# Output pieces of a state-space layer started one a slot, four gate blocks side by side, and one silu for the later columns

## The chip, the cores and the metric

The kernel runs on one core of a Trainium2 chip. The metric is device time in microseconds (us) of one execution; less is better. Three runs of the kernel before took 902.46 to 907.09 us, with a median of 904.3 us.

## What is computed

Two residual layers over 256 tokens of width 2048, in float32. Layer 0 is grouped-query attention and lies outside the change. Layer 1 is a bidirectional diagonal state-space layer, cut here to what matters:

```python
u, z = split(h @ w_in, 2)                       # 2 x 2048 columns
y = scan_fwd(u) + scan_bwd(u) + d_skip * u      # 128 groups of 16 channels, 64 complex states
g = gelu(y)
y = g * sigmoid(g @ w_glu + b_glu)
y = y * silu(z)
x = layer_norm(alpha * x + y @ w_out)
```

## The kernel before, in words

Every product is made from three reduced-precision ones: the weights are loaded in **chunks** of 512 KB (`raw`, L157, on SP's DMA queue), ScalarE (ACT) rounds a chunk to its high part `wh` (L146), GpSimd (POOL) or VectorE (DVE) takes the difference `wl` (L148), and TensorE (PE) runs 24 matmuls on it (`chunk_ch`, L209 to L211). `plan1` writes down the order of the chunks of layer 1: 16 blocks of 128 columns of u, 16 of z, 8 blocks of 256 columns of the gate `w_glu`, then `w_out`.

After each chunk the kernel calls `step()`, so a **slot** is one chunk of matmuls. In a slot each lane (`in`, `scan`, `out`, `g`, `glu`) may start waiting tasks, up to its width, and moves its live tasks on by one `yield`. `until(test)` calls `step()` without a chunk until the test holds. This fixes the order in which instructions are written; the framework then makes each engine's queue from it, and may pull an instruction forward that it takes for ready while the engine would be idle.

Layer 1 goes as follows. Blocks of u go out to DRAM and come back in another layout; `in_task` turns them into the scan's input `V`. The scan (`scan_task`, L888 to L890 on DVE) runs in two batches, pieces 0 to 7 and 8 to 15 (`BATCH`), 62 columns each, 3 columns a slot. Meanwhile PE makes the z blocks, and ACT puts silu on each (L1034) into `z1`.

`OUT_LAG` slots after a batch's last column its eight `out_task`s are queued; the lane's width is `OUT_W` = 2. A piece's task starts with the copies of the forward and backward states into `su` (L908 on ACT; L909 on ACT for pieces 0 to 7, on DVE for 8 to 15) and the loads of `om` (L913) and `up` (L918). At every fourth piece it also loads the Toeplitz block `tr` with eight DMAs (L495) and turns it into `tt` with two ACT copies (L498). Two slots later come 48 small matmuls into `yps` (L933), one slot after that gelu (L938) into `yg`, which is written to `Gd` by ACT's queue (L939). A `g_task` reads `Gd` back as `gp` (L953, SP's queue), and five slots later splits it into the two parts of `gT` (L243 on ACT, L244 on DVE).

The gate's matmuls need `gT`: chunk c of a block needs pieces 4c to 4c+3. Before, the first two gate blocks run chunks 0 to 2 each, then wait for pieces 12 to 15, then run their chunks 3; the other six blocks run whole. `glu_task` adds sigmoid (L963) and the products with `z1` (L966 to L968).

Buffers that the text speaks of: `su` and `tr` share the tag `q4` (4 slots), `om` and the scan's input `im` share `im` (`NIM` = 2), `tt` has one buffer, `yps` three PSUM banks, `yg` two. Loads of `up` and `gp` and the write of `Gd` are 128 KB each.

Of the kernel before, what the change touches and what calls it, by code (L numbers as in the profile page):

```python
# [9 lines left out]
F32 = mybir.dt.float32  # L10
F32R = mybir.dt.float32r
I32 = mybir.dt.int32
AF = mybir.ActivationFunctionType
# [5 lines left out]
S = 256  # L19
D = 2048  # L20
KB = D // 128
# [4 lines left out]
C = 16  # L26
NP = 64
L = 4
# [3 lines left out]
NB = G // GB  # L32
PG = 8
NPIECE = G // PG
# [6 lines left out]
class Trunk:  # L41
# [153 lines left out]
        self.step()  # L195
        return parts

    def chunk_ch(self, ps, act, c):

        self.feed()  # L200
        nc, (ah, al) = self.nc, act
        wh, wl = self.parts.pop(self.cur)
        n = wh.shape[1]
        for kk in range(n):
            kb = n * c + kk
            for i in range(len(ps)):
                f = slice(i * 128, i * 128 + 128)
                o = ps[i][:, :S]
                nc.tensor.matmul(o, lhsT=wh[:, kk, f], rhs=ah[:, kb], start=kb == 0, stop=False)  # L209
                nc.tensor.matmul(o, lhsT=wh[:, kk, f], rhs=al[:, kb], start=False, stop=False)  # L210
                self.mm = nc.tensor.matmul(o, lhsT=wl[:, kk, f], rhs=ah[:, kb], start=False, stop=kb == KB - 1).ins  # L211
        self.cur += 1
        self.step()

# [272 lines left out]
    def toeplitz(self, b):  # L487

        nc, wk = self.nc, self.wk1
        raw = wk.tile([128, L, 16, C], F32, tag="q4", name="tr", bufs=self.Q4)  # L490
        with self.tc.issue_after(self.paced):
            for h in range(2):
                for tau in range(L):
                    src = self.Kd[b, h, :, 3 - tau:7 - tau].rearrange("c j e -> c (j e)")
                    nc.sync.dma_start(raw[h * 64 + tau:h * 64 + 64:L].rearrange("q j a e -> q (j a e)"), src)  # L495
        t = wk.tile([128, 16, C, L], F32, tag="tt", name="tt")
        for a in range(2):
            nc.scalar.copy(t[:, a * 8:a * 8 + 8], raw[:, :, a * 8:a * 8 + 8].rearrange("q t a e -> q a e t"))  # L498
        return t

    def columns(self, pool):
# [290 lines left out]
    def plan1(self):  # L792
        a = self.a
        W, WG, WO = a["w_in_ssm"][0], a["w_glu"][0], a["w_out_ssm"][0]
        self.first = len(self.chunks)
        self.plan_ch(W, 0)
        for b in range(2, 32):
            self.plan_one(W, b * 128)
        for b in range(2):
            self.plan_ch(WG, b * 256, 0, 3)  # L800
        for b in range(2):
            self.plan_ch(WG, b * 256, 3, 4)
        for b in range(2, 8):
            self.plan_ch(WG, b * 256)
        for nb in range(4):
            self.plan_tok(WO, nb * 512, nb == 3)
# [71 lines left out]
    def scan_task(self, p0, p1):  # L878

        v = self.nc.vector  # L880
        n, g0 = (p1 - p0) * PG, p0 % 8 * PG
        V = self.V[p0 // 8][:, :, :, g0:g0 + n]
        cf = self.coef[:, :, :, p0 * PG:p1 * PG]
        shp = [128, 2, 2, n]
        for c in range(1, NCH - 1):
            P = self.sc.tile([128, 512], F32, tag="scp", name="scp")[:, :4 * n].rearrange("q (e r g) -> q e r g", e=2, r=2)
            with self.urgent():
                v.tensor_tensor(P, cf, V[:, c - 1].unsqueeze(1).to_broadcast(shp), ALU.mult)  # L888
                v.tensor_tensor(V[:, c], V[:, c], P[:, 0], ALU.add)
                self.swept = v.tensor_tensor(V[:, c], V[:, c], P[:, 1, ::-1], ALU.add).ins  # L890
            yield
        t = self.now + self.OUT_LAG
        while self.now < t:
            yield
        for pc in range(p0, p1):
            self.add("out", self.out_task(pc))

    def out_task(self, pc):

        nc, v, wk = self.nc, self.nc.vector, self.wk1  # L900
        b, q = pc // 4, pc % 4
        V = self.V[pc // 8]
        gs = slice(pc % 8 * PG, pc % 8 * PG + PG)
        su = wk.tile([128, 2, PG, NCH], F32, tag="q4", name="su", bufs=self.Q4)
        f, r = slice(0, 64), slice(64, 128)
        nc.gpsimd.memset(su[f, :, :, 0:1], 0.0)
        nc.gpsimd.memset(su[r, :, :, NCH - 1:], 0.0)
        nc.scalar.copy(su[f, :, :, 1:], V[f, 0:NCH - 1, :, gs].rearrange("p s r g -> p r g s"))  # L908
        (v.tensor_copy if pc >= 8 else nc.scalar.copy)(su[r, :, :, :NCH - 1], V[r, NCH - 2::-1, :, gs].rearrange("p s r g -> p r g s"))  # L909
        self.flags.add(("su", pc))  # L910
        tag, bufs = ("im", self.NIM) if self.n_in == NPIECE and self.OMT else ("q4", self.Q4)
        om = wk.tile([128, 2, PG, C * L], F32, tag=tag, name="om", bufs=bufs)
        nc.sync.dma_start(om, self.OMd[pc])  # L913
        if q == 0:
            self.tt = self.toeplitz(b)
        tt = self.tt
        up = wk.tile([128, 4, NCH], F32, tag="up", name="up2", bufs=3)
        nc.sync.dma_start(up, self.Ud[pc].rearrange("h c t a k -> (h c t) a k"))  # L918
        yield
        yield  # L920
        ps = self.pm.tile([128, 512], F32, tag="pm", name="yps", bufs=self.npm)

        h = [slice(g % 2 * 64, g % 2 * 64 + 64) for g in range(PG)]
        o = [ps[h[g], g // 2 * NCH:g // 2 * NCH + NCH] for g in range(PG)]
        even, odd = range(0, PG, 2), range(1, PG, 2)
        jobs = [(g, None) for g in even] + [(g, ri) for ri in range(2) for g in range(PG)] + [(g, None) for g in odd]
        seen = set()
        with ExitStack() as order:
            for n, (g, ri) in enumerate(jobs):
                lhsT = tt[h[g], q * 4 + g // 2].rearrange("q e t -> q (e t)") if ri is None else om[:, ri, g]  # L930
                rhs = up[h[g], g // 2] if ri is None else su[:, ri, g]
                stop = ri is None if g % 2 else ri == 1
                m = nc.tensor.matmul(o[g], lhsT=lhsT, rhs=rhs, start=g % 2 not in seen, stop=stop, skip_group_check=True)  # L933
                seen.add(g % 2)
                order.enter_context(self.tc.issue_after(m.ins))
        yield
        yg = wk.tile([128, 4, NCH], F32, tag="yg", name="yg", bufs=2)
        nc.scalar.activation(yg.rearrange("p a k -> p (a k)"), ps[:, :S], AF.Gelu_apprx_tanh)  # L938
        nc.scalar.dma_start(self.Gd[pc].rearrange("(a h) c t k -> (h c t) a k", h=2), yg)  # L939
        self.add("g", self.g_task(pc), *[("su", p) for p in range(8)])  # L940
# [49 lines left out]
    def layer1(self, out):  # L990
        nc, v = self.nc, self.nc.vector
# [11 lines left out]
        h = (hT[:, 0], hT[:, 1])  # L1003
        ps = self.banks()
# [19 lines left out]
        for b in range(2, NPIECE):  # L1024
            if "open" not in self.flags and (self.idle("prep") or b == self.OPEN):
                self.open(ssm)
            ps = self.block_ch(h)
            self.taken(b, ps[0])
            self.add("in", self.in_task(b), "open")
        s2, wk = self.s2, self.wk1  # L1030
        self.z1 = self.mid.tile([128, KB, S], F32, tag="mid", name="z1")
        for b in range(NPIECE):
            ps = self.block_ch(h)
            nc.scalar.activation(self.z1[:, b], ps[0][:, :S], AF.Silu)  # L1034
        self.until(lambda: self.idle("scan"))
        self.psum(4)

# [1 line left out]
        act = (self.gT[:, 0], self.gT[:, 1])  # L1039
        yT = self.s0.tile([128, 2, KB, S], F32R, tag="s0", name="y2T")  # L1040
        y = (yT[:, 0], yT[:, 1])
        need = lambda c: self.until(lambda: all(("g", p) in self.flags for p in range(4 * c, 4 * c + 4)))
        two, gains = [self.banks(), self.banks()], []
        for ps in two:
            for c in range(3):
                need(c)
                self.chunk_ch(ps, act, c)
        need(3)
        for b in range(8):
            if b < 2:  # L1050
                ps = two[b]
                self.chunk_ch(ps, act, 3)
            else:
                ps = self.block_ch(act)
            if b >= 4:
                gains.append(wk.tile([128, 2, 512], F32, tag="q4", name="gains", bufs=self.Q4))
                self.load_gains(gains[-1], 0, b - 4)
            for i in range(2):
                self.add("glu", self.glu_task(2 * b + i, ps[i][:, :S], y))
        ready = lambda c: all(("y", f) in self.flags for f in (2 * c, 2 * c + 1))  # L1060
        src = lambda i, cs: [(0, 128, self.h1d[i, :, cs])]
        for nb in range(4):
            res = self.residual(nb, src, gains[nb])
            gains[nb] = wk.tile([128, 2, 512], F32, tag="q4", name="gains2", bufs=self.Q4)
            self.load_gains(gains[nb], 1, nb)
            if nb == 3:
                break
            ps = self.block_tok(y, ready)
# [39 lines left out]
            self.layer1(out)  # L1108

    Q4 = 4  # L1110
    JOIN = (1, 0)
    FIN = (('V', 'gg', 'gg', 'gg'), ('V', 'gg', 'vv', 'vv'))
    ONE = 0
# [11 lines left out]
    GLAG = 5  # L1125
    POOL = (1, 70)
    OUT_W = 2
    OUT_E = 1
    OMT = 1
    IN_EVERY = 1  # L1130
# [1 line left out]
    EACH = 2  # L1132
    NRAW = 4
    HP = 0
    NIM = 2
    BUDGET = 8
    OUT_LAG = 4
    IN_LAG = 1
    BATCH = (8, 16)
    NWH = 4  # L1140
# [48 lines left out]
```

## Time and profile before

| | us |
|---|---|
| median of three runs | 904.3 |
| the profiled execution | 909.47 |
| its span, first to last instruction | 907.5 |
| scan of the state-space layer, DVE | 509.8 to 648.8 |
| last block of z done on PE | 679.4 |
| gate matmuls on PE | 681.0 to 804.2 |

The profile is of one execution. Busy time is the union of an engine's instructions; an "idle before" time is put down to what ended it. The granted clock of TensorE is a share of 2.4 GHz. The times of windows, timelines and chains count from the span's start.

### The profile page before, as it was taken

To read this page: it belongs to the slowest core of one execution; us is meant where nothing else is said; L and a number is where in the kernel's file an instruction comes from. 1 tells how busy PE (TensorE), PEld (TensorE's weight loads), DVE (VectorE), ACT (ScalarE), POOL (GpSimd) and SP (SyncE) were. 2 spreads that over 40 slices of the span, in tenths; PEclk is the share of its full clock that TensorE was granted. 3 is DMA by queue.
4 is the path that set the end of the run, shared out by engine and by line. 5 is a ranking of instruction groups with operands and counts; after the bars stand their busy time and mean duration, and the time that the engine had idled before them with its cause. 6 is when DMAs were issued, how large, how long until landed. Compare 5 with 4: busy or idle time off the path is not lost.

```text
span 907.5 us, 18418 instructions
## 1 busy us (share of the span) xinstructions
PE 841.0 (93%) x7244; PEld 763.8 (84%) x7244; DVE 651.8 (72%) x1178; ACT 519.9 (57%) x743; POOL 262.7 (29%) x182
## 2 busy tenths in 40 slices
PE   5999999999999898997889999998998789999993
PEld 4788989889899687886889999987897789998882
DVE  3999899999979977987200498899732477766646
ACT  3554467768668564454456566489968554543321
POOL 0008500000002222334556666744584000000004
PEclk9999999999999999998999999997999979999997
DMA  9765588776757658987789989774797946786733
GB/s 235 235 193 176 141 254 265 204 194 217 203 180 205 192 157 240 234 284 232 215 233 282 274 246 301 208 208 140 212 277 238 298 133 203 232 242 215 246 92 92
DMA packets 217798, 195.82 MB, mean 216 GB/s; under 512 B 67648, under 2 KB 174064, under 8 KB 217456
## 3 DMA queue, kind: packets, MB, share of 16 engines
q1 hardware_dynamic: 200688, 189.93, 70.3%
q10 hardware_dynamic: 17024, 4.72, 2.2%
q8 instruction: 57, 0.93, 0.4%
q14 instruction: 29, 0.24, 0.1%
HBM read 168.39 MB, written 26.21 MB: 214 GB/s over the span
## 4 chain that ended last, share of the span: by engine, by line
PE 64%; DMA 16%; DVE 8%; ACT 4%; issue 4%; SPq 2%; POOL 1%; ACTq 0%; DVEq 0%; POOLq 0%
PE acc L185 9%; PE acc L186 9%; PE acc L184 9%; PE acc L209 9%; PE acc L210 9%; PE acc L211 9%; DMA Ud<-ut 3%; DMA om<-OMd 2%; PE yps L933 2%; DMA up<-Ud 1%; DMA Gd<-yg 1%; PE kps L459 1%; DMA h1d<-r 1%; ACT su L908 1%; PE imps L441 1%
## 5 line engine op out<-in xcount | busy, mean ns | idle before, releaser
L146 ACT CAST wh<-raw 128x1024 fp32r<-128x1024 f32 x234 | 245.0, 1050 | 219.7 <-PE acc L186 74.1
L148 POOL TENSOR_TENSOR wl<-raw,wh 128x1024 fp32r<-128x1024 f32 x84 | 207.9, 2480 | 359.1 <-ACT wh L146 340.4
L148 DVE TENSOR_TENSOR wl<-raw,wh 128x1024 fp32r<-128x1024 f32 x150 | 187.7, 1255 | 54.9 <-ACT wh L146 54.4
L209 PE MATMUL acc<-h1T,wh 128*128 128x256 f32 x512 | 148.3, 294 | 3.2 <-ACT ut L841 3.2
L210 PE MATMUL acc<-h1T,wh 128*128 128x256 f32 x512 | 147.0, 288 | 0.0
L211 PE MATMUL acc<-h1T,wl 128*128 128x256 f32 x512 | 146.5, 287 | 0.1
L888 DVE TENSOR_TENSOR scp<-cf,V 128x256 f32<-128x256 f32 x124 | 53.6, 432 | 77.6 <-ACT V L875 73.4
L209 PEld LDWEIGHTS acc<-h1T,wh 128*128 128x128 f32 x512 | 99.6, 197 | 5.3 <-ACT ut L841 3.4
L211 PEld LDWEIGHTS acc<-h1T,wl 128*128 128x128 f32 x512 | 100.5, 196 | 0.3 <-POOL wl L148 0.3
L210 PEld LDWEIGHTS acc<-h1T,wh 128*128 128x128 f32 x512 | 100.7, 197 | 0.0
L184 PE MATMUL acc<-wh,xT 128*128 128x512 f32 x192 | 75.6, 399 | 2.8 <-ACT wh L146 2.6
L209 PE MATMUL acc<-gT,wh 128*128 128x256 f32 x256 | 71.0, 287 | 6.9 <-ACT gT L243 6.1
L185 PE MATMUL acc<-wl,xT 128*128 128x512 f32 x192 | 76.0, 396 | 0.8 <-DVE wl L148 0.8
L186 PE MATMUL acc<-wh,xT 128*128 128x512 f32 x192 | 76.2, 397 | 0.0
L211 PE MATMUL acc<-xT,wl 128*128 128x256 f32 x256 | 73.0, 286 | 0.0
L210 PE MATMUL acc<-xT,wh 128*128 128x256 f32 x256 | 72.9, 285 | 0.0
L210 PE MATMUL acc<-gT,wh 128*128 128x256 f32 x256 | 72.9, 287 | 0.1
L209 PE MATMUL acc<-xT,wh 128*128 128x256 f32 x256 | 72.7, 284 | 0.0
L211 PE MATMUL acc<-gT,wl 128*128 128x256 f32 x256 | 72.1, 284 | 0.0
L1096 POOL TENSOR_TENSOR r<-r,gains 128x512 f32<-128x512 f32 x8 | 11.0, 1401 | 183.6 <-ACT r L1094 183.5
L209 PEld LDWEIGHTS acc<-gT,wh 128*128 128x128 f32 x256 | 48.2, 193 | 7.7 <-ACT gT L243 6.6
L184 PE MATMUL acc<-wh,oT 128*128 128x512 f32 x128 | 51.0, 406 | 2.8 <-ACT wh L146 2.8
(254 smaller groups left out, 1901.5 us busy)
## 6 DMA issues: line engine op xcount, KB each, us to landing
raw<-in_w_in_attn_dram SPq DMA_DIRECT2D x80, 512.0 KB, 5.0
raw<-in_w_in_ssm_dram SPq DMA_DIRECT2D x64, 512.0 KB, 6.8
raw<-in_w_out_attn_dram SPq DMA_DIRECT2D x32, 512.0 KB, 4.8
raw<-in_w_glu_dram SPq DMA_DIRECT2D x32, 512.0 KB, 4.4
raw<-in_w_out_ssm_dram SPq DMA_DIRECT2D x32, 512.0 KB, 4.9
IMd<-im SPq DMA_DIRECT2D x16, 512.0 KB, 6.6
OMd<-om SPq DMA_DIRECT2D x16, 512.0 KB, 6.2
im<-IMd SPq DMA_DIRECT2D x16, 512.0 KB, 7.3
```

The costliest lines, as they stand in the source:

```text
L146: nc.scalar.copy(wh, raw)
L148: (nc.gpsimd if i - self.first in range(*self.POOL) or i in self.POOL0 else nc.vector).tensor_tensor(wl, raw, wh.bitcast(F32), ALU.subtract)
L184: nc.tensor.matmul(ps, lhsT=xh, rhs=wh[:, kk], start=kb == 0, stop=False)
L185: nc.tensor.matmul(ps, lhsT=xh, rhs=wl[:, kk], start=False, stop=False)
L186: nc.tensor.matmul(ps, lhsT=xl, rhs=wh[:, kk], start=False, stop=kb == KB - 1)
L209: nc.tensor.matmul(o, lhsT=wh[:, kk, f], rhs=ah[:, kb], start=kb == 0, stop=False)
L210: nc.tensor.matmul(o, lhsT=wh[:, kk, f], rhs=al[:, kb], start=False, stop=False)
L211: self.mm = nc.tensor.matmul(o, lhsT=wl[:, kk, f], rhs=ah[:, kb], start=False, stop=kb == KB - 1).ins
L441: nc.tensor.transpose(ps[:, q * 128:q * 128 + 128], X[:, ri, 2 * pr:2 * pr + 2].rearrange("q g c t -> q (g c t)"), self.ident)
L888: v.tensor_tensor(P, cf, V[:, c - 1].unsqueeze(1).to_broadcast(shp), ALU.mult)
L933: m = nc.tensor.matmul(o[g], lhsT=lhsT, rhs=rhs, start=g % 2 not in seen, stop=stop, skip_group_check=True)
L1096: (nc.gpsimd if k == "g" else v).tensor_tensor(x, x, o, op)
```

## The change

- `chunk_ch` gets `one`: the two 128-column halves of a gate block share one PSUM bank (512 float32 columns), so only the first matmul of the bank starts it.
- Four gate blocks instead of two are held open, one bank each, and their chunks go rows outermost: chunk 0 of blocks 0 to 3, chunk 1 of the four, chunk 2 of the four; then the wait for pieces 12 to 15; then their chunks 3. `plan1` writes the chunks in that order.
- After the second batch of the scan the out lane's width becomes 4, and the lag is 1 slot instead of 4 (`OUT_LAG = (4, 1)`).
- The Toeplitz block of the next four pieces is loaded at the second piece of a block and turned at its fourth; odd blocks are turned into two buffers of the tag `res`.
- `NIM` becomes 3.
- From block `ZB` = 7 on, z is copied without silu; one silu over blocks 7 to 15 (2304 columns) stands behind the wait for pieces 12 to 15.

```diff
-    def chunk_ch(self, ps, act, c):
+    def chunk_ch(self, ps, act, c, one=False):
...
-                nc.tensor.matmul(o, lhsT=wh[:, kk, f], rhs=ah[:, kb], start=kb == 0, stop=False)
+                nc.tensor.matmul(o, lhsT=wh[:, kk, f], rhs=ah[:, kb], start=kb == 0 and not (one and i), stop=False, skip_group_check=one)
...
+        return raw
+
+    def turned(self, b, raw):
+        if b % 2:
+            t = [self.wkr.tile([128, 8, C, L], F32, tag="res", name="tt", bufs=4) for _ in range(2)]
+        else:
+            whole = self.wk1.tile([128, 16, C, L], F32, tag="tt", name="tt")
+            t = [whole[:, a * 8:a * 8 + 8] for a in range(2)]
         for a in range(2):
-            nc.scalar.copy(t[:, a * 8:a * 8 + 8], raw[:, :, a * 8:a * 8 + 8].rearrange("q t a e -> q a e t"))
+            self.nc.scalar.copy(t[a], raw[:, :, a * 8:a * 8 + 8].rearrange("q t a e -> q a e t"))
         return t
...
-        for b in range(2):
-            self.plan_ch(WG, b * 256, 0, 3)
-        for b in range(2):
-            self.plan_ch(WG, b * 256, 3, 4)
-        for b in range(2, 8):
+        for c in range(4):
+            for b in range(4):
+                self.plan_ch(WG, b * 256, c, c + 1)
+        for b in range(4, 8):
             self.plan_ch(WG, b * 256)
...
-        t = self.now + self.OUT_LAG
+        t = self.now + self.OUT_LAG[p1 == NPIECE]
         while self.now < t:
             yield
+        if p1 == NPIECE:
+            self.lanes["out"]["width"] = self.OUT_W2
...
-        if q == 0:
-            self.tt = self.toeplitz(b)
-        tt = self.tt
+        if pc == 0:
+            self.tt = {0: self.turned(0, self.toeplitz(0))}
+        if q == 1 and b < NB - 1:
+            self.tr = self.toeplitz(b + 1)
+        if q == 3 and b < NB - 1:
+            self.tt[b + 1] = self.turned(b + 1, self.tr)
+        tt = self.tt[b]
...
-            nc.scalar.activation(self.z1[:, b], ps[0][:, :S], AF.Silu)
+            if b < self.ZB:
+                nc.scalar.activation(self.z1[:, b], ps[0][:, :S], AF.Silu)
+            else:
+                nc.scalar.copy(self.z1[:, b], ps[0][:, :S])
...
-        two, gains = [self.banks(), self.banks()], []
-        for ps in two:
-            for c in range(3):
-                need(c)
-                self.chunk_ch(ps, act, c)
+        halves = lambda p: [p[:, :S], p[:, S:]]
+        four, gains = [halves(p) for p in self.banks(4)], []
+        for c in range(3):
+            need(c)
+            for ps in four:
+                self.chunk_ch(ps, act, c, True)
         need(3)
+        nc.scalar.activation(self.z1[:, self.ZB:], self.z1[:, self.ZB:], AF.Silu)
         for b in range(8):
-            if b < 2:
-                ps = two[b]
-                self.chunk_ch(ps, act, 3)
+            if b < 4:
+                ps = four[b]
+                self.chunk_ch(ps, act, 3, True)
...
+    ZB = 7
+    OUT_W2 = 4
-    NIM = 2
+    NIM = 3
-    OUT_LAG = 4
+    OUT_LAG = (4, 1)
```

## Rows read from the trace of the kernel before

**Rows 1.** The page: TensorE's share of the span, and its granted clock in 40 slices.
```profile
PE 841.0 (93%) x7244; PEld 763.8 (84%) x7244; DVE 651.8 (72%) x1178; ACT 519.9 (57%) x743; POOL 262.7 (29%) x182
...
PEclk9999999999999999998999999997999979999997
```
**Rows 2.** Windows: length, busy us (instructions) by engine, then granted clock, DMA share, GB/s.
```profile
594.00:649.00 55.00, 47.63 (x529) 45.12 (x528) 49.70 (x149) 51.06 (x41) 21.76 (x18) 0.91 0.57 170
649.00:681.00 32.00, 31.14 (x318) 29.59 (x317) 13.41 (x10) 22.05 (x32) 28.27 (x19) 1.00 0.87 262
681.00:731.00 50.00, 39.01 (x529) 36.41 (x530) 17.67 (x23) 33.50 (x38) 11.95 (x12) 0.92 0.84 261
731.00:742.00 11.00, 10.94 (x71) 10.64 (x71) 7.97 (x18) 6.49 (x12) 0.00 (x0) 0.75 0.21 69
742.00:804.20 62.20, 62.20 (x531) 62.20 (x530) 47.24 (x73) 30.79 (x46) 0.00 (x0) 1.00 0.72 219
```
**Rows 3.** Groups of ACT in 598 to 649 us: busy us, mean ns | idle before.
```profile
L908 ACT COPY su<-V 64x1008 f32<-64x1008 f32 x8 | 16.2, 2020 | 0.1
L909 ACT COPY su<-V 64x1008 f32<-64x1008 f32 x8 | 15.8, 1977 | 0.1
...
L938 ACT ACT_TABLE_LOAD x3 | 3.8, 1283 | 0.1
L1034 ACT ACT_TABLE_LOAD x2 | 2.6, 1283 | 0.0
```
**Rows 4.** Timeline of ACT: a table load and the silu behind it.
```profile
624.43 1.28 ACT L1034 ACT_TABLE_LOAD   x1
625.73 0.38 ACT L1034 ACTIVATE z<-acc 128x256 f32<-128x256 f32 x1
```
**Rows 5.** Waits of PE in 594 to 742 us: total us, times, longest.
```profile
PE acc L209 <- ACT gT L243: 6.1, 2, 3.2
PE yps L933 <- ACT tt L498: 5.5, 2, 3.6
PE yps L933 <- ACT yg L938: 4.0, 1, 4.0
```
**Rows 6.** Timeline of DVE: the scan's last instruction.
```profile
648.52 0.29 DVE L890 TENSOR_TENSOR V<-V,scp 128x128 f32<-128x128 f32 x1
```
**Rows 7.** The chain that ended last, after the scan: start, us, what.
```profile
686.05 6.31 DMA om<-OMd
...
710.36 8.56 DMA om<-OMd
...
720.85 0.39 ACT yg L938
721.27 7.48 DMA Gd<-yg
728.81 1.87 DMA gp<-Gd
```
**Rows 8.** Timeline of ACT behind the last z block.
```profile
680.86 7.67 ACT L908 COPY su<-V 64x1008 f32<-64x1008 f32 x4
```
**Rows 9.** Timeline of PE: the matmuls of one output piece.
```profile
612.72 0.67 PE L933 MATMUL yps<-up,tt 64*64 64x64 f32 x8
...
614.41 0.68 PE L933 MATMUL yps<-up,tt 64*64 64x64 f32 x8
```
**Rows 10.** DMA issues in 590 to 745 us: count, KB each, median us to landing.
```profile
om<-OMd SPq DMA_DIRECT2D x14, 512.0 KB, 5.1
...
Gd<-yg ACTq DMA_DIRECT2D x16, 128.0 KB
...
tr<-Kd SPq DMA_DIRECT2D x24, 64.0 KB, 4.7
```
**Rows 11.** Groups of ACT in 649 to 731 us: the rounding of weight chunks and of `gp`.
```profile
L146 ACT CAST wh<-raw 128x1024 fp32r<-128x1024 f32 x16 | 16.6, 1045 | 7.8 <-PE acc L210 3.3 <-DMA raw<-in_w_glu_dram 1.6 <-POOL su L906 1.3
...
L243 ACT CAST gT<-gp 128x256 fp32r<-128x256 f32 x16 | 6.0, 402 | 5.0 <-DMA gp<-Gd 4.7
```

More of the change, by code (lines that the diff above doesn't have):

```diff
@@ L208, in chunk_ch @@
                 o = ps[i][:, :S]
-                nc.tensor.matmul(o, lhsT=wh[:, kk, f], rhs=ah[:, kb], start=kb == 0, stop=False)
-                nc.tensor.matmul(o, lhsT=wh[:, kk, f], rhs=al[:, kb], start=False, stop=False)
-                self.mm = nc.tensor.matmul(o, lhsT=wl[:, kk, f], rhs=ah[:, kb], start=False, stop=kb == KB - 1).ins
+                nc.tensor.matmul(o, lhsT=wh[:, kk, f], rhs=ah[:, kb], start=kb == 0 and not (one and i), stop=False, skip_group_check=one)
+                nc.tensor.matmul(o, lhsT=wh[:, kk, f], rhs=al[:, kb], start=False, stop=False, skip_group_check=one)
+                self.mm = nc.tensor.matmul(o, lhsT=wl[:, kk, f], rhs=ah[:, kb], start=False, stop=kb == KB - 1, skip_group_check=one).ins
         self.cur += 1
@@ L495, in toeplitz @@
                     nc.sync.dma_start(raw[h * 64 + tau:h * 64 + 64:L].rearrange("q j a e -> q (j a e)"), src)
-        t = wk.tile([128, 16, C, L], F32, tag="tt", name="tt")
+        return raw
[5 more added lines that the diff above has]
+            t = [whole[:, a * 8:a * 8 + 8] for a in range(2)]
         for a in range(2):
-            nc.scalar.copy(t[:, a * 8:a * 8 + 8], raw[:, :, a * 8:a * 8 + 8].rearrange("q t a e -> q a e t"))
+            self.nc.scalar.copy(t[a], raw[:, :, a * 8:a * 8 + 8].rearrange("q t a e -> q a e t"))
         return t
@@ L929, in out_task @@
             for n, (g, ri) in enumerate(jobs):
-                lhsT = tt[h[g], q * 4 + g // 2].rearrange("q e t -> q (e t)") if ri is None else om[:, ri, g]
+                lhsT = tt[q // 2][h[g], q % 2 * 4 + g // 2].rearrange("q e t -> q (e t)") if ri is None else om[:, ri, g]
                 rhs = up[h[g], g // 2] if ri is None else su[:, ri, g]
```

## The prediction, made before the result was known

> **What bounds the kernel now.** I read the page first: TensorE is busy for 93% of the span, so the kernel is matmul-bound except where the engine waits, and the clock line shows where that is: two slices fall to 7 in the stretch in which layer 1's outputs are made [rows 1]. Then the windows of that stretch [rows 2]. In 742 to 804.2 us TensorE is busy throughout at clock 1.00, 531 matmuls in 62.2 us, so a chunk of 24 costs 24 x 62.2 / 531 = 2.8 us there. Ahead of it are two bad stretches. Stretch A, 594 to 649, is idle for 55.0 - 47.6 = 7.4 us at clock 0.91. Stretch C, 681 to 731, is idle for 11.0 us at 0.92, and the 11 us behind it still run at 0.75. A mean of 0.91 between the levels 2.4 and 1.2 GHz means 0.18 x 55 = 9.9 us at the lower one. Time at the lower level costs half of itself where the engine works: at most 5.0 us in A, at most 4.0 us in C (I take 2, since much of it lies in idle time), and 0.25 x 11 = 2.8 us after C.
>
> Then who ends the waits [rows 5]. The gate's matmuls wait 6.1 us for `gT`; the pieces' matmuls wait 5.5 us for `tt` and 4.0 us for a gelu. In A the engine behind this is ACT: it is busy 51.1 of 55 us [rows 2], of which 32.0 us are the sixteen `su` copies and 6.4 us are five table loads, since gelu of the pieces and silu of z take turns [rows 3]. In C it is a chain: the scan ends at 648.8 [rows 6], but ACT's `su` copies for pieces 8 and on stand behind the last z block, four in a row from 680.9 on [rows 8]; `om` loads of 6.3 and 8.6 us, then the last gelu at 720.9, its write of 7.5 us and read of 1.9 us follow [rows 7], and TensorE has no other work by then.
>
> **The slots, counted from the code.** Slot 0 is the first chunk of layer 1. The second batch's input is complete at slot 34; 62 columns at 3 a slot end at slot 55; z ends at slot 64. Before: lag 4, so piece 8 starts at 59; a task lives 4 slots and two may live, so piece 15 starts at 72, its gelu is written at 75, its split at 81. Only six gate chunks may run ahead of that, so the waits insert 12 slots with no chunk in them. After: lag 1, piece 8 at 57; width 4 equals the life of 4 slots, so one piece starts in every slot, piece 15 at 64, gelu at 67, split at 79 (now the `g` lane sets that). Twelve gate chunks run ahead, and the waits insert 4 empty slots. In written order nearly all of the wait is covered: six more chunks are 16.8 us, more than the chain of 10 us from the last gelu to the read's landing [rows 7].
>
> **Stretch A: the silu.** Block 7 is done at slot 48, just after the first gelu, so from there on z is a plain copy, and no table changes until the end. Of the five loads in A [rows 3] only the first one to gelu is left: four go. A load takes 1.28 us, and the next instruction begins 1.30 us after it [rows 4]: 4 x 1.30 = 5.2 us of ACT. ACT is the bound there, so TensorE gets them: **-5.2 us**. Bounds: 0 if another wait takes over, -12.4 if all idle and slow time goes.
> The Trainium skill (ScalarE: Activation LUTs, What ACT_TABLE_LOAD costs) gives 1283 ns and about 1380 ns of drain, 2.66 us for a switch. The load agrees with the row, the drain does not show in 1.30 us; by that rule this term would be -10.6 us.
>
> Toeplitz loads: 24 DMAs move from every fourth piece to two or three pieces earlier, into time where the DMA share is 0.57 [rows 2]; the two copies `tt` move with them on ACT, same sum. The wait of 5.5 us for `tt` goes [rows 5]; 3.6 us of it lie in C and are counted there. Against this, `tr` now takes one of the four `q4` slots during two pieces of `su`: at worst a piece's matmuls wait once more for two copies, 4.0 us [rows 3]. I take zero, because ACT makes the copies one after another anyhow.
>
> **Stretch C.** Removable: idle 0.9 + 11.0, clock 2 and 2.8, together 16.7 us [rows 2]. What limits a slot now? TensorE: a chunk and a piece, 2.8 + 2.2 (48 matmuls, the first begun at 612.72, the last ended at 615.09, of which 0.2 us run on beside the next) = 5.0 us [rows 9]. ACT: 2.0 for `su`, 1.05 and 0.40 for the roundings, 0.38 each for gelu and half a z block: at most 4.2 us [rows 3, 4, 11]. It fits. DMA: slots 57 to 67 hold 10 chunks and 9 pieces, 47.4 us, and must move 10 chunks and 8 `om` of 512 KB, 26 transfers of 128 KB (`up`, `Gd`, `gp`) and one `tr` of 512 KB, 13.4 MB [rows 10]: 283 GB/s. The best window has 262 GB/s at share 0.87 with TensorE never waiting [rows 2]; at that rate the stretch takes 51.1 us. I charge these **+3.7 us**; between 0 (the share may rise to 0.94) and +31 (at 170 GB/s, the lowest row).
> The Trainium skill (DMA: Bandwidth & Descriptors, Where 436 GB/s comes from) puts the limit from memory at about 358 GB/s for a core; no window here shows it held, and by it this charge would be zero.
>
> The one silu over 2304 columns: 256 columns take 0.38 us and a rounding of 1024 takes 1.05 us [rows 4, 11], so some 2.2 us, plus a load. If it stands where it is written, the first sigmoids come some 3.5 us later, while TensorE has the next three chunks 3, 8.4 us: nothing. But it is ready after the last z block, and the queue may take it forward between two gelus, where it costs 2.2 + 2 x 1.3 = 4.8 us of ACT. I charge half, **+2.4 us**. Four chunks 3 in a row bring `glu` work of eight tasks to DVE at once; it is idle for 15 of 62 us in the gate [rows 2]: nothing, or 2 us if weights' `wl` come late. `NIM` = 3 lets one more `im` or `om` load run early: 0 to -1. The shared bank is read only after both halves end: nothing.
>
> C together: -16.7 + 3.7 + 2.4 = **-10.6 us**. Sum: -5.2 - 10.6 = -15.8 us. The profiled execution took 909.5 us, so it becomes 893.7; it was 5.2 us above the median, and against the median of 904.3 the forecast is **888.5 us**.
>
> **Rivals.**
> *Half of it.* The framework's queues keep the old order: the `su` copies stay behind the last z block and the buffers, not the lane, set the pace. Then the `tt` wait of 3.6 us and the clock's 2 us go, A gives nothing: 904.3 - 5.6 = 898.7. For it: four `q4` slots for three live `su` and a `tr`, none spare. Against: even with copies from 680.9 on, eight pieces at 4.2 us of ACT end at 714.5, ahead of now.
> *A new wait in A cancels the gain.* `tr` holding a `q4` slot delays pieces 2 and 3 by 4.0 us each, and the slow clock after it costs some 2 us more: +10, against -10.6 in C: 904. For it: ACT has 4 us of 55 left there.
> *Slower: the DMA queue.* Place: slots 57 to 67 on SP's queue, where `raw` stands behind `om` and `tr`. Starved weights stop TensorE. At 170 GB/s [rows 2] 13.4 MB take 78.8 us, 31.4 more than planned, against -5.2 - 16.7 + 2.4 = -19.5: 916. It decides from 188 GB/s down, where 71.3 us eat 19.5 + 4.5. Against it: 261 and 262 GB/s were held in the nearest windows; 170 stands where little was asked.
>
> **How the numbers follow.** A measurement of this kernel can tell 0.5% (4.5 us) from no change. Forecast 0.60 (879 to 898), half 0.20 (895 to 902, three quarters of it beyond 0.5%), cancelled 0.12, slower 0.08. Faster 0.60 + 0.15 = 0.75, with 0.01 of the cancelled case 0.76; same 0.16; slower 0.08. The low end, 879, has A at -9 and C nearly whole; the high end, 902, holds the half case. Left out: slower, half of the cancelled case, and a few in a hundred below.
>
> **What would show it.** Right: one gelu table load and no silu load between 620 us and the end of the pieces; ACT's `su` copies for 8 to 15 some 5 us apart and begun ahead of the last z block; clock 1.00 from the first gate chunk on; no wait for `gT` or `tt`; gate matmuls ending some 16 us earlier at the same length behind. Wrong: idle time of TensorE in A as before with ACT full, PE waiting for `om` or for `wl` in the pieces' slots, or the combined silu among gelus with a piece late behind it.

## The result and the profile after

The changed kernel takes 895.2 us (median of four runs, 894.2 to 896.0), the kernel before, beside it on the same chip, 905.7 (four runs, 902.5 to 908.4): a ratio of 0.9864, 95% interval 0.9833 to 0.9895. That is 12.3 us by the ratio and 10.5 by the medians, where 15.8 were forecast. The profiled execution took 895.47 us, its span 893.7, TensorE's mean clock 0.977 (909.47, 907.5 and 0.970 before; that execution lies 3.8 us above its median beside the change, so the leads read from the two profiles add up to 13.8).

The size is near the forecast, the places are not. The table gives five moments of TensorE, each the start of a matmul read from the timeline, and the end of the span.

| | before | after | lead | won in this stage | forecast |
|---|---|---|---|---|---|
| first matmul of u in layer 1 | 421.8 | 420.7 | 1.1 | 1.1 | 0 |
| first matmul of the scan's input (`vps`) | 456.3 | 449.7 | 6.6 | 5.5 | 0 |
| first matmul of an output piece (`yps`) | 594.5 | 586.5 | 8.0 | 1.4 | 0 |
| last matmul of z | 679.4 | 670.7 | 8.7 | 0.7 | 5.2 |
| last matmul of the gate | 804.2 | 789.7 | 14.5 | 5.8 | 10.6 |
| end of the span | 907.5 | 893.7 | 13.8 | -0.7 | 0 |

More than half of the lead is there before the first output piece starts, in stages that the prediction didn't look at. Two profiles also differ by chance: no edit in this document touches the code ahead of the table's first line, and over its fourteen profiles that moment lies between 416.7 and 421.8 us. So a stage is read from several profiles below where that is possible.

These are the windows of the changed kernel that answer to [rows 2], with one of the u stage ahead of them; the columns are length, busy us (instructions) of PE, PEld, DVE, ACT and POOL, granted clock, DMA share, GB/s.

```profile
440.00:480.00 40.00, 38.69 (x588) 37.52 (x586) 0.00 (x0) 22.60 (x26) 27.05 (x12) 1.00 0.87 250
594.00:649.00 55.00, 48.46 (x567) 46.07 (x566) 49.59 (x131) 49.38 (x46) 25.96 (x23) 0.94 0.67 198
649.00:681.00 32.00, 28.70 (x336) 27.01 (x335) 12.29 (x11) 19.33 (x23) 22.67 (x18) 0.95 0.92 287
681.00:731.00 50.00, 46.72 (x507) 44.95 (x506) 22.80 (x27) 30.29 (x37) 6.02 (x4) 0.90 0.73 224
731.00:742.00 11.00, 11.00 (x96) 11.00 (x95) 6.63 (x10) 7.19 (x12) 0.00 (x0) 1.00 0.58 193
```

The same first window in the kernel before:

```profile
440.00:480.00 40.00, 33.97 (x467) 32.94 (x468) 0.00 (x0) 18.98 (x24) 23.79 (x11) 0.91 0.84 241
```

In 440 to 480 us TensorE is now busy 38.69 us at full clock instead of 33.97 at 0.91. In 594 to 649 it gains under 1 us. In 681 to 731 it works 46.72 us instead of 39.01, but at 0.90: the slow clock is still there.

The waits of TensorE in 580 to 790 us of the changed kernel, which answer to [rows 5] (waiting tile, what released it, total us, times, longest):

```profile
PE yps L947 <- ACT yg L952: 7.3, 2, 4.0
PE yps L947 <- ACT su L918: 2.9, 1, 2.9
PE yps L947 <- ACT su L919: 2.5, 2, 2.1
PE yps L947 <- DMA up<-Ud: 0.4, 1, 0.4
```

The waits for `gT` (6.1 us) and `tt` (5.5 us) are gone, as forecast. What is left are waits of pieces for ACT: for a gelu, twice 3.3 to 4.0 us, and for `su`.

**The first gelu wait, in stretch A.** ACT's timeline in the changed kernel, then the matmul that waits (start, us; in brackets the idle time ahead of it):

```profile
609.61 2.03 ACT L918 COPY su<-V 64x1008 f32<-64x1008 f32 x1
611.65 1.90 ACT L919 COPY su<-V 64x1008 f32<-64x1008 f32 x1
613.57 1.28 ACT L952 ACT_TABLE_LOAD   x1
614.87 0.38 ACT L952 ACTIVATE yg<-yps 128x256 f32<-128x256 f32 x1
...
615.30 0.68 PE L947 MATMUL yps<-up,tt 64*64 64x64 f32 x8 [4.00 <-ACT yg L952]
```

The only table load that is left in A stands behind two more `su` copies, and TensorE waits for the gelu after it.

**The second, in stretch C.** Where ACT's `su` copies for pieces 8 and on stand now, which answers to [rows 8]:

```profile
671.94 7.47 ACT L918 COPY su<-V 64x1008 f32<-64x1008 f32 x4
```

They still come four in a row behind the last matmul of z. ACT and TensorE some 10 us later:

```profile
682.11 0.37 ACT L952 ACTIVATE yg<-yps 128x256 f32<-128x256 f32 x1
682.50 1.28 ACT L1067 ACT_TABLE_LOAD   x1
683.80 2.12 ACT L1067 ACTIVATE z<-z 128x2304 f32<-128x2304 f32 x1
...
685.83 1.88 ACT L918 COPY su<-V 64x1008 f32<-64x1008 f32 x1
687.72 1.28 ACT L952 ACT_TABLE_LOAD   x1
689.02 0.38 ACT L952 ACTIVATE yg<-yps 128x256 f32<-128x256 f32 x1
...
689.45 1.11 PE L947 MATMUL yps<-up,tt 64*64 64x64 f32 x8 [3.29 <-ACT yg L952]
```

The late silu is not where it is written, behind the wait for pieces 12 to 15: it was taken forward between two gelus, with a table load on either side, 4.7 us of ACT in all. TensorE's eight matmuls behind the wait take 1.11 us instead of 0.67 [rows 9], and just after them the granted clock is 0.50, the lower of the two levels (1.2 of 2.4 GHz):

```profile
691.00:696.00 5.00, 5.00 (x50) 4.54 (x47) 0.30 (x1) 3.94 (x6) 2.36 (x1) 0.50 0.35 90
```

The window's 0.90 means 0.2 x 50 = 10 us at this level in 681 to 731 us.

### The profile page after: what moved, and what is told of

Same layout as the page of the kernel before. It is cut to its first block, busy times and chain, and to the rows that moved or that the text cites. A ratio compares the mean times of both kernels' runs of the same rounds, so it can differ in the third digit from the quotient of the medians.

```text
span 893.7 us, 18431 instructions
## 1 busy us (share of the span) xinstructions
PE 836.7 (94%) x7244; PEld 759.5 (85%) x7244; DVE 654.6 (73%) x1178; ACT 513.9 (58%) x738; POOL 262.2 (29%) x182
## 4 chain that ended last, share of the span: by engine, by line
PE 62%; DMA 14%; DVE 9%; ACT 5%; issue 5%; SPq 3%; POOL 1%; ACTq 0%; DVEq 0%; POOLq 0%
PE acc L184 10%; PE acc L185 10%; PE acc L186 10%; PE acc L210 8%; PE acc L211 8%; PE acc L212 8%; DMA Ud<-ut 5%; PE yps L947 2%; DMA up<-Ud 1%; PE kps L460 1%; SPq L496 1%; PE vps L879 1%; ACT su L918 1%; DMA raw<-in_w_in_ssm_dram 1%; DMA Gd<-yg 1%
## 5 line engine op out<-in xcount | busy, mean ns | idle before, releaser
L210 PEld LDWEIGHTS acc<-h1T,wh 128*128 128x128 f32 x512 | 98.2, 194 | 4.2 <-ACT ut L849 1.6
L211 PEld LDWEIGHTS acc<-h1T,wh 128*128 128x128 f32 x512 | 99.2, 194 | 0.2 <-DVE h1T L844 0.2
L185 PE MATMUL acc<-wl,oT 128*128 128x512 f32 x128 | 51.0, 400 | 0.0
```

Of the source, the lines that this page charges most:

```text
L185: nc.tensor.matmul(ps, lhsT=xh, rhs=wl[:, kk], start=False, stop=False)
```

## The experiments

All are timed beside the kernel before; its pooled medians in the three sessions were 906.7 (25 runs), 906.4 (13 runs) and 906.7 us (9 runs).

| | median us (lowest to highest, runs) | ratio to before, 95% interval |
|---|---|---|
| the change | 895.2 (894.2 to 896.0, 4) | 0.9864 [0.9833, 0.9895] |
| e7: two `im` buffers | 897.9 (892.6 to 902.3, 10) | 0.9903 [0.9866, 0.9940] |
| e1: e7, `tt` out of `res` | 904.4 (898.0 to 907.0, 10) | 0.9962 [0.9933, 0.9991] |
| e2: before, reads of `h1d` behind the newest weights | 905.1 (902.8 to 907.9, 10) | 0.9980 [0.9953, 1.0007] |
| e9: before, reads behind the first z weights | 907.3 (902.2 to 913.4, 10) | 0.9998 [0.9960, 1.0037] |
| e3: the change, late silu held back | 888.1 (885.1 to 890.4, 4) | 0.9795 [0.9743, 0.9846] |
| e4: the change, no late silu | 895.8 (889.3 to 897.3, 4) | 0.9840 [0.9745, 0.9936] |
| e5: e3, two gate blocks | 888.2 (884.7 to 892.3, 4) | 0.9772 [0.9695, 0.9850] |
| e6: e3, old out lane | 883.4 (880.9 to 888.1, 4) | 0.9724 [0.9647, 0.9801] |
| e10: e3, both old | 889.0 (884.8 to 895.6, 4) | 0.9806 [0.9754, 0.9858] |
| e11: before, Toeplitz part alone | 899.4 (896.9 to 902.4, 4) | 0.9905 [0.9872, 0.9938] |
| e13: before, held late silu alone | 902.3 (898.6 to 905.2, 6) | 0.9941 [0.9915, 0.9967] |
| e12: e6, half of `su` on GpSimd | 891.5 (888.9 to 892.5, 4) | 0.9822 [0.9793, 0.9851] |

### Where the lead of the u stage comes from: e7, e1, e2, e9

The timeline of SyncE's queue in the kernel before, at the start of layer 1:

```profile
423.08 0.58 SPq L1020 DMA_DIRECT2D h1d<-r  x1
433.91 0.32 SPq L764 DMA_DIRECT2D res<-h1d  x1
434.33 0.38 SPq L1020 DMA_DIRECT2D h1d<-r  x1
434.81 0.38 SPq L157 DMA_DIRECT2D raw<-in_w_in_ssm_dram  x1
439.93 0.32 SPq L764 DMA_DIRECT2D res<-h1d  x1
```

and the wait that the waits of this queue show for it (415 to 460 us):

```profile
SPq L764 <- DMA h1d<-r: 15.0, 2, 10.2
```

Layer 1's input is written to DRAM (`h1d`), and read back for the residual at the kernel's very end. The buffers `res` for it were free, so the framework pulled these reads forward by more than 200 us, right behind the write that they need. SyncE's queue then stood for 15.0 us, with the weight loads behind it. In the changed kernel the odd Toeplitz blocks occupy `res`, and the reads start at 660.8 and 700.7 us; the wait is gone. e7 asks whether it is the third `im` buffer instead; e1 gives the odd blocks buffers of their own, so that `res` is free as before.

```diff
# e7
-    NIM = 3
+    NIM = 2
# e1, on top of e7
-            t = [self.wkr.tile([128, 8, C, L], F32, tag="res", name="tt", bufs=4) for _ in range(2)]
+            t = [self.wkr.tile([128, 8, C, L], F32, tag="odd", name="tt", bufs=2) for _ in range(2)]
```

> The changed kernel with NIM back at 2. Its trace leads the kernel before by 6.6 us at the first matmuls of the scan's input (449.7 against 456.3 us), ahead of everything that the prediction priced. Theory A (reads of h1d no longer stand in SP's queue there, since res buffers are taken by tt): nothing lost in that stretch, 894 to 897 us. Rival B (the third im buffer gave that lead): about 7 us lost, 902 us, the first matmuls of the scan's input back at 456 us.

> The same with NIM 2, and the turned Toeplitz blocks of odd number in a tag of their own instead of res, so that the residual's reads of h1d find their buffers free early, as before. Theory A: those reads go back into SP's queue near 430 us and wait for the write of h1d, weights behind them are late, 6 to 8 us more than with res: 901 to 904 us. Rival B, or plain variation between executions: no difference from the run with NIM 2 alone.

With two `im` buffers the lead stays: the scan's input starts at 450.7 us, 29.0 us after the first u matmul, as in the change. With `res` free the wait is back (SyncE's waits, 415 to 460 us, of e1),

```profile
SPq L773 <- DMA h1d<-r: 14.7, 2, 9.7
```

the stage takes 33.5 us, and the kernel 6.5 us longer than e7 by the medians (904.4 against 897.9 us) and 5.3 by the ratios, whose intervals overlap by 0.0007; the ten runs of each, compared directly, differ by 5.4 us in the mean (95% interval 2.3 to 8.6). Over all profiles, the first u matmul to the first `vps` takes 33.5 to 35.0 us in the three kernels that have this wait (before, e1, e13) and 29.0 to 31.7 in the eleven that don't. So the lead of this stage comes from reads that the change displaces without meaning to. What the third `im` buffer brings, 2.8 us by the medians of the change and e7, is not resolved by their intervals.

Is it enough, then, to hold these reads back in the kernel before? e2 issues them behind the latest weight load, e9 behind the weight load that is latest when z begins.

```diff
# e2
-                nc.sync.dma_start(t[o:o + n], ap)
+                with self.tc.issue_after(self.paced) if gains is not None else ExitStack():
+                    nc.sync.dma_start(t[o:o + n], ap)
# e9: the same with self.mark, set ahead of the loop over the z blocks
+        self.mark = self.paced
```

> The kernel before, with one edit: the residual's reads of h1d are issued behind the latest weight load of their place in the program. Theory A: 6 to 8 us faster than the kernel before, 898 to 900 us, with no part of the change in it. Rival B or variation: 905 to 906 us.

> The kernel before, with the residual's reads of h1d issued behind the weight load that is latest when the z blocks begin, so early enough for the end and out of the way of the first blocks. Theory A: the 7 us of the first blocks stay to the end, 898 to 901 us. Rival (the waits of the stages behind, for tt, gelu and gT, take the lead back): 903 to 906 us.

It is not. Both have the shorter u stage (29.4 and 29.2 us), and neither is measurably faster. In e2 the reads come too late; in its last stage VectorE waits for them (790 to 910 us):

```profile
DVE res L767 <- DMA res<-h1d: 17.3, 4, 6.6
```

Before, this wait is 6.0 us, and the stage from the last gate matmul to the end takes 103.3 us, 105.8 in e2. Another 3.7 us go between the first output piece and the last z (88.6 us against 84.9). In e9 the last stage is as long as before (103.8 us), and nothing is gained either. The waits of TensorE in 580 to 742 us of e9 show one that has grown:

```profile
PE yps L934 <- ACT tt L498: 8.9, 2, 5.5
PE acc L209 <- ACT gT L243: 4.2, 2, 2.5
```

and so does its window of stretch A (same columns as the windows above):

```profile
594.00:649.00 55.00, 46.90 (x501) 44.67 (x499) 46.34 (x127) 52.18 (x47) 23.11 (x20) 0.84 0.62 183
```

The wait for `tt` is 8.9 us instead of 5.5 [rows 5], and the clock in A 0.84 instead of 0.91 [rows 2]. This profile is the fastest of e9's ten runs, so it doesn't size the loss.

### The late silu: e3, e4

e3 issues it behind ACT's last rounding of `gT`; e4 leaves it out and puts silu on every block as before.

```diff
# e3 (in the split of gT, and in front of the late silu)
-        self.nc.scalar.copy(h, src)
+        self.rounded = self.nc.scalar.copy(h, src).ins
...
-        nc.scalar.activation(self.z1[:, self.ZB:], self.z1[:, self.ZB:], AF.Silu)
+        with self.tc.issue_after(self.rounded):
+            nc.scalar.activation(self.z1[:, self.ZB:], self.z1[:, self.ZB:], AF.Silu)
# e4, on the change
-    ZB = 7
+    ZB = 16
-        nc.scalar.activation(self.z1[:, self.ZB:], self.z1[:, self.ZB:], AF.Silu)
```

> The changed kernel with the one silu over the later columns held behind the last rounding of gT on ACT. Theory C (taken forward between two gelus, with a table load on either side, it costs 4.7 us of ACT, a wait of 3.5 us on PE and some 3 us at half the clock): 5 to 7 us faster, 888 to 890 us, no wait on gelu at 686 us. Rival D (the pieces' chain has slack or waits next for su copies or om): within 2 us of 895.

> The changed kernel with silu on every z block as before and no late one. To be read against the kernel with the late silu held (888.1 us). Theory E (the prediction's first term: ACT is the bound in 594 to 649, and each pair of table loads between silu and gelu is on the path): 5 us or more above it, 893 to 896 us, so about as slow as the changed kernel, whose late silu costs as much as it saves. Rival F (the loads lie in time that ACT has to spare): 887 to 890 us.

e3 takes 888.1 us, 7.1 below the change (6.3 by the ratios, whose intervals overlap by 0.0013), and no run of the one reaches into those of the other. Stretch C of e3:

```profile
681.00:731.00 50.00, 49.42 (x563) 48.23 (x561) 26.00 (x34) 32.17 (x42) 4.92 (x4) 1.00 0.80 248
```

TensorE is idle for 0.6 us of it and at full clock. From the last matmul of z to the last of the gate the profile has 112.2 us, 119.0 in the change. So the late silu in the wrong place costs some 7 us. The windows of 681 to 731 us account for it: 3.3 us idle against 0.6, and 10 us at half the clock, which cost up to 5. e4 is no slower than the change: where it stands, the late silu costs what it saves. Against e3, e4's ratio is 0.0045 higher (4.1 us; 7.7 by the medians); their intervals overlap, but its groups of ACT in 594 to 731 us have nine table loads for gelu and silu, as before, where e3 has one for gelu and one for the late silu:

```profile
L952 ACT ACT_TABLE_LOAD x5 | 6.4, 1283 | 0.1
L1049 ACT ACT_TABLE_LOAD x4 | 5.1, 1283 | 0.5 <-ACT yg L952 0.4
```

### One piece a slot and four gate blocks: e5, e6, e10

On e3, these set back the gate's order, the lane, and both.

```diff
# e5: plan1 and layer1 as before for the gate, two blocks held open
-        for c in range(4):
-            for b in range(4):
-                self.plan_ch(WG, b * 256, c, c + 1)
+        for b in range(2):
+            self.plan_ch(WG, b * 256, 0, 3)
...
-        four, gains = [halves(p) for p in self.banks(4)], []
+        four, gains = [halves(p) for p in self.banks(2)], []
# e6
-    OUT_W2 = 4
+    OUT_W2 = 2
-    OUT_LAG = (4, 1)
+    OUT_LAG = (4, 4)
# e10: both
```

> The changed kernel with the late silu held and two gate blocks open instead of four, column by column as before. By the slots, the last piece is split at slot 79 while six gate chunks end at slot 70. Theory G (rows outermost covers the chain behind the last pieces): 6 to 10 us above 888.1, 894 to 898 us, with waits for gT again. Rival H (with one piece a slot the chain is short enough): 888 to 890 us.

> The changed kernel with the late silu held, and the out lane back at width 2 and lag 4. The last split then stands at slot 81 with twelve chunks before it. Theory G (the cover matters more than the lane): 2 to 5 us above 888.1, 890 to 893 us. Rival (the lane is the part that pays): 8 us or more, 896 us and up.

> The held version (late silu behind the last rounding of gT) with both the two gate blocks and the old out lane (width 2, lag 4): what is left of the change is the Toeplitz part, the late silu and the third im buffer. Alone, two blocks gave 888.2 and the old lane 883.4 against 888.1. Theory (the two are covers for the same wait: either one suffices, both away bring the wait for gT back): 891 to 896, with PE waits for gT of 4 us or more. Rival (neither matters once ACT's queue is free of table loads): 883 to 889, waits for gT under 2 us.

The rival of e10 is what came: under 2 us of waiting for `gT`, and a time at its upper edge. The four medians are 888.1, 888.2, 883.4 and 889.0 us, the intervals all overlap, and the profiled spans of e3, e6 and e10 are 883.3, 883.4 and 883.0 us; e5's is 890.5, but its profile is the slowest of its four runs. The two parts from which the prediction had nearly all of C's gain show no gain, each alone and both together; the intervals of 5 to 7 us either way leave room for a small one. e6 has the lowest median of all, 883.4, and beats both kernels; that it is better than e3 is not shown. The wide lane does bring a wait of its own: in all six kernels that have it (the change, e7, e1, e3, e4, e5) TensorE waits 2.9 us for the first `su` behind the last matmul of z, and in e6 and e10 it doesn't.

Why they are not needed is seen in e10, whose gate runs in the old order behind the old lane. Its waits of TensorE in 580 to 742 us, from the longest, are

```profile
PE yps L948 <- ACT su L920: 2.4, 2, 2.1
PE acc L212 <- POOL wl L148: 1.9, 1, 1.9
PE acc L211 <- DVE gT L245: 1.8, 1, 1.8
```

The wait for ACT's part of `gT`, 6.1 us before, is gone; 1.8 us for DVE's part are left. So six chunks of work in front of pieces 12 to 15 are nearly enough, once these pieces are not late.

### Each of the two other parts alone: e11, e13

```diff
# e11, on before: toeplitz, turned and tt in out_task as in the change's diff
+        if pc == 0:
+            self.tt = {0: self.turned(0, self.toeplitz(0))}
+        if q == 1 and b < NB - 1:
+            self.tr = self.toeplitz(b + 1)
+        if q == 3 and b < NB - 1:
+            self.tt[b + 1] = self.turned(b + 1, self.tr)
# e13, on before: ZB = 7 and the late silu held as in e3
```

> The kernel before with the Toeplitz part alone: loads at a block's second piece, the two copies at its fourth, odd blocks in the residual's buffers; lag, width, gate blocks, silu and im buffers as before. Theory T (this part carries the lead of the u stage, because the residual's reads of h1 can't start early any more, and removes the wait for tt): pieces' matmuls begin near 450 us instead of 456, no PE wait for tt, and the time falls by 5 to 10 us to 897 to 902. Rival (the lead is taken back further on by the chain to gT): the lead is seen at 456 but the time is 904 to 908.

> The kernel before with the late silu alone, issued behind the last rounding of gT as in the held version; nothing else changed. Theory (table loads lie on ACT's path while pieces 0 to 7 go out): four table loads less in 594 to 649 us, and 4 to 7 us less time, 900 to 903. Rival (before, the pieces wait for other things, tt and the chain to gT, so that ACT's time is not what ends it): 905 to 908.

The Toeplitz part alone brings 8.6 us by its ratio (1 - 0.9905, of 906.7; interval 5.6 to 11.6), the held silu 5.3 (3.0 to 7.7). Both times are those that the theories gave. In e11's trace the wait for `tt` is gone and the scan's input starts at 451.4 us, as its theory says. In e13's one of five table loads is left in 594 to 649 us, but the gain is not where the theory puts it: from the first output piece to the last matmul of the gate the profile has 208.7 us, 209.7 before, and 4.0 of its lead of 6.9 us are there at the first matmul of u, ahead of anything that it edits. What makes e13 faster is therefore not shown.

The waits of e11 (580 to 742 us), from the longest:

```profile
PE acc L209 <- ACT gT L243: 6.1, 2, 4.2
PE yps L945 <- ACT yg L950: 2.6, 1, 2.6
```

and of e13:

```profile
PE yps L933 <- ACT tt L498: 6.5, 2, 3.5
PE acc L209 <- ACT gT L243: 5.7, 2, 3.3
```

Each leaves the wait for ACT's part of `gT` about as it was, 6.1 and 5.7 us; with both (e10) it is gone. From the first output piece to the last matmul of the gate the profiles have 209.7 us before, 209.3 in e11, 208.7 in e13 and 195.2 in e10: in this stretch each part alone brings next to nothing, and both together 14.5 us. Two delays, of table loads between gelus and of pieces that wait for `tt`, both feed the chain that ends in `gT`, so that taking away one leaves the other; that fits, but it is argued. By the times, e10 gains 17.6 us (12.9 to 22.3) where the two alone sum to some 14, which doesn't prove an excess. And e10 has the third `im` buffer and the shared PSUM banks too, which were not tried apart: the change and e7, with three and two `im` buffers, differ by 4.3 us in this stretch (203.2 and 207.5).

### Is stretch A bound by ACT? e12

The prediction took ACT for the bound of 594 to 649 us. e12 takes the backward half of the `su` copies of pieces 0 to 7 off ACT.

```diff
# e12, on e6
-        (v.tensor_copy if pc >= 8 else nc.scalar.copy)(su[r, ...
+        (v.tensor_copy if pc >= 8 else nc.gpsimd.tensor_copy)(su[r, ...
```

> The held version with the old out lane, and the backward half of su for pieces 0 to 7 copied by GpSimd instead of ACT: some 16 us of copies leave ACT in 594 to 649 us. Theory (ACT still bounds that stretch): TensorE's idle time and slow time there go, 2 to 5 us less than the 883.4 of the version without this, 878 to 882. Rival (GpSimd makes such a copy much slower than ACT's 2.0 us, and the weights' differences, which it makes too, come late): 884 to 892.

It takes 891.5 us, 8 more than e6, and the runs of the two don't overlap. The windows of stretch A, first e6, then e12:

```profile
594.00:649.00 55.00, 50.81 (x565) 48.32 (x564) 48.79 (x127) 48.15 (x45) 25.28 (x23) 0.88 0.69 200
```

```profile
594.00:649.00 55.00, 47.84 (x538) 44.69 (x537) 41.70 (x123) 28.79 (x35) 36.41 (x29) 0.88 0.71 203
```

ACT fell from 48.15 to 28.79 us, and TensorE worked 3 us less. The copy itself is no slower on GpSimd; its group in 594 to 649 us of e12 (busy us, mean ns | idle before):

```profile
L919 POOL COPY su<-V 64x1008 f32<-64x1008 f32 x7 | 13.6, 1963 | 0.1
```

The waits of SyncE's queue (594 to 652 us) and of ACT (594 to 649 us) show what is late instead:

```profile
SPq L923 <- PE yps L947: 20.3, 6, 7.0
SPq L967 <- DMA Gd<-yg: 15.9, 4, 5.4
...
ACT wh L146 <- DMA raw<-in_w_in_ssm_dram: 13.5, 3, 7.4
```

SyncE's queue stands 20.3 us at `om` loads whose buffer the pieces' matmuls still hold (7.6 us in e6), and 15.9 us at reads of `Gd` whose write isn't done (6.7 in e6); the weight loads are behind them in the same queue, so ACT waits 13.5 us for weights, and its gelus come behind them: TensorE's longest wait here, 3.7 us, is for a gelu. The rival's time came about, but not by its first reason: GpSimd takes 1.96 us a copy, as ACT does. So an ACT that is full is not the only thing that holds A. That GpSimd's later weight differences have a part in the 8 us was not separated.

## Why the prediction was right, and where it was not

The time lies in the range and the sign is right, but in good part by luck. The sum, -15.8 us against a measured -10.5 to -12.3, comes from terms that were off in both directions, and a lead that no term contained made up for them. Without that lead, 6.5 us by e7 and e1, the changed kernel would take some 901.7 us by this estimate, at the upper end of the range (902); e1, which has neither it nor the third `im` buffer, takes 904.4.

- **The u stage and the scan, 0 forecast, 8.0 us in the profile.** The step that failed: "Toeplitz loads: 24 DMAs move ..." with "I take zero". It asked where the moved loads go, and not what the buffers held that the odd blocks are turned into. The reads that lost their place had held SyncE's queue for 15.0 us, over 150 us ahead of the first piece. By e7 and e1 this is worth 6.5 us within the change (5.3 by the ratios).
- **Stretch A, -5.2 forecast, 0.7 in the profile.** The count was right: one load instead of five, and the next instruction starts 1.30 us after a load begins (682.50 to 683.80). "ACT is the bound there, so TensorE gets them" was the failing step: a gelu that stands behind two `su` copies on ACT still stopped TensorE for 4.0 us, and e12 shows a second bound behind ACT. By itself, with the silu held, the edit is worth 5.3 us of kernel time (e13), with seven loads for gelu and silu fewer in 594 to 731 us (nine before, two in e13), but its profile has only 1.0 us of that in the stretch of the pieces and the gate. The Trainium skill (ScalarE: Activation LUTs, What ACT_TABLE_LOAD costs), with its 2.66 us for a switch, would have given an estimate of 10.6 us for four; no run here shows as much.
- **Stretch C, -10.6 forecast, 5.8 in the profile.** "I charge half, +2.4" is the term that was mis-sized: the late silu was taken forward, which the prediction named and priced at 4.8 us of ACT, and it cost 7 us (e3), since the slow clock behind the wait came on top. Of "Removable 16.7", e3 got 12.6 us: 124.8 us from the end of z to the end of the gate before, 112.2 there. But what removed it was not the lane or the four blocks (e5, e6, e10); the cover that the slot count gave them was not needed. This stage takes 122.6 us with the early `tt` alone (e11), 125.2 with the held silu alone (e13), and 111.2 with both (e10).
- **The DMA charge, +3.7.** It wasn't paid. 649 to 681 us moved 287 GB/s, above the 262 that it was worked out from, and e3 fills stretch C at 248. The Trainium skill (DMA: Bandwidth & Descriptors, Where 436 GB/s comes from) by its limit of about 358 GB/s would have charged nothing, as the prediction says, and that was right here. The 262 was not the best window either: the kernel before moves 277 with TensorE nearly always busy (columns as in [rows 2]):

```profile
480.00:500.00 20.00, 19.91 (x324) 19.20 (x323) 0.00 (x0) 11.44 (x15) 12.92 (x6) 1.00 0.93 277
```

- **The signs to look for.** No wait for `gT` or `tt`, and the gate's end 14.5 us earlier (16 forecast): seen. Clock 1.00 from the first gate chunk: not seen, 0.90. The `su` copies begun ahead of the last z block and 5 us apart: not so. Four stand in a row from 671.94 us on, 1.2 us after the last matmul of z (1.5 us before), and the first is the wait of 2.9 us above. They stand ahead of the last copy of z, but no earlier against TensorE.
- **The rivals.** The half case had the copies where they were, A giving nothing and C 5.6 us, at 898.7. The profile has 0.7 and 5.8, so stage by stage it was nearer than the forecast, though what held C was the late silu (e3) and not the buffers that it named; the time came out lower since the u stage, which no case had, gave its lead. Neither the cancelled nor the slower case happened: TensorE has no wait for weights in 580 to 790 us of the changed kernel, though e12 shows that SyncE's queue can make ACT wait for them. Waits for a `q4` slot are there, on GpSimd, which fills the edges of `su`: 5.8 us for pieces' matmuls and 0.9 for `tt` in 580 to 742 us, against 3.5 and 10.0 before; ACT's copies of `su` don't wait for it.

Left open: where e13's gain comes from, and why e2 and e9 lose their lead where e11 keeps it. The longer wait for `tt` is seen in one profile; holding the reads and turning the Toeplitz blocks early in two separate steps, with `res` left alone, was not tried.

## What to carry to other kernels

When an edit takes over a buffer, ask what used to be put there and when: one of the two largest effects here came from reads that the framework had pulled forward into a free buffer, onto a queue that weights share. (In the kernel before, holding these reads back did not pay by itself.) An instruction whose data is ready early may be taken forward; if it changes the activation table, tie it to the last of the work that it must not interrupt. And before building cover for a late chain, take away what makes it late: with the table loads and the `tt` wait gone, the reordered gate and the wider lane showed no gain.

## What the runs showed of the hardware that was not expected

- A read of DRAM that stands in SyncE's queue behind the write it depends on blocks the queue, for 10.2 us at the longest here, and everything behind it: the next weight load was issued 0.9 us after the first such read went out.
- A copy 64x1008 of the scan's states takes 1.96 us on GpSimd (e12) and 1.98 to 2.02 us on ACT [rows 3].
- The misplaced silu takes 4.7 us of ACT and shows as one stop of TensorE of 3.3 us, but the change is 6.8 us longer than e3 from the end of z to the end of the gate, with the granted clock at 0.90 against 1.00 in 681 to 731 us.
